# Seven products for the gate and up halves in all four layers, weight sums by adding transfers, result sums in a pre-filled bank

## The chip, the cores and the metric

One Trainium2 chip, and of it one core. The metric is the device time of one execution in microseconds (us). A core has five engines that run beside each other: TensorE (PE) multiplies matrices, VectorE (DVE) and ScalarE (ACT) work element by element, GpSimd (POOL) does small vector work and can issue transfers, SyncE (SP) issues the transfers from main memory. PSUM is the accumulator that TensorE writes: eight banks of 128 x 512 floats. SBUF is the on-chip store that all engines read.

## What is computed

A stack of four layers over 512 tokens of 1024 channels, in float32. Each layer has a mixer (attention and the like), a norm, and a feed-forward part. Only the feed-forward part matters here. Layers 0 and 1 use the first form, layers 2 and 3 the second:

```
def _swiglu(x, w_gate, w_up, w_down):                 # layers 0, 1
    g = jnp.einsum('bsd,df->bsf', x, w_gate)          # 1024 -> 2816
    u = jnp.einsum('bsd,df->bsf', x, w_up)
    return jnp.einsum('bsf,fd->bsd', jax.nn.silu(g) * u, w_down)

def conv_ffn(h, w_up, cw, cb, w_down):                # layers 2, 3
    gu = causal_dwconv(h @ w_up, cw, cb)              # 3 taps along the tokens, per channel
    g, u = jnp.split(gu, 2, axis=-1)
    return (jax.nn.gelu(g, approximate=True) * u) @ w_down
```

## The kernel before

**Arithmetic.** Every product is made of three passes on TensorE: an operand is split into a high half (rounded to the matmul's type) and a low half (the rest), and high x high, high x low and low x high are summed. A block of weights of 128 x 1024 (512 KB) is loaded by SP into a `wraw` buffer (six of them); ScalarE casts it to `whi` (L245), VectorE subtracts to get `wlo` (L246), both with four buffers. `fm` makes one output tile of 128 channels by some tokens from such a block: 8 steps of 128 rows, three passes each, 24 matmuls.

**Layers 2 and 3** use `ffn` (L1308 on): 22 tiles f of 128 hidden channels, each a gate and an up product over 512 tokens, so 44 products of 24 matmuls of 512 columns. For each of the two, ScalarE scales and adds the bias (L1332, Identity), VectorE adds the two shifted taps (L1334, twice); then ScalarE applies Gelu (L1337) and VectorE multiplies (L1338). The first two tiles go through `early`, in halves of 256 tokens, so that they can start before the last tokens are normed.

**Layers 0 and 1** use `quartered`: two neighbouring tiles and both halves of the tokens form a 2 x 2 block problem, in which blocks b11, b12, b21, b22 of the weights meet a11, a12, a21, a22 of the activations, and seven products take the place of eight. There are 11 such units in a layer. One product is 24 matmuls of 256 columns (two groups of 12). Products 1, 2 and 3 use the blocks b11, b21 and b22 as loaded; 4 to 7 use sums of blocks, made by four VectorE additions of 128 x 1024 in each unit (L524). Results gather in three banks, and VectorE forms their differences (L590 to L608) before `finish` applies Silu and the product (L550).

**The seven activation operands** of such a layer are made by `crossed`, one token tile t of 128 at a time: TensorE transposes the normed tile, VectorE and ScalarE split it. For t = 2 and 3, which are the second half of the tokens, the sums of both halves are made and split too (L478 to L487): nine VectorE steps of 128 x 512 for each. This runs at the end of the mixer's last product, beside the norm, and reaches into the first products of the feed-forward part: the work of the last tokens is put off (`later`) and issued behind the third product.

**What sets the order.** There is no planner: each engine executes what is written for it, in program order, and waits on semaphores for what it needs. SP's loads are issued in program order as `wraw` buffers come free. In a unit of layers 0 and 1 the products come as 1, 5, then 3 and 4 of the unit before, 7, 2, 6. No transfer is issued by POOL; POOL computes the power -1/2 of the norms (L410, L1362, on 128 x 1 elements).

Of the kernel before, what the change touches and what calls it, by code (L numbers as in the profile page):

```python
# [30 lines left out]
PAD = 56  # L31
LAG = 1
# [14 lines left out]
BANKS = {"mm": 2, "o": 1, "sc": 3, "tp": 2}  # L47
TOKEN_BANKS = (("mm", "mm"), ("o", "tp"), ("tp", "sc"), ("sc", "sc"))
# [61 lines left out]
def layouts(a):  # L110
# [35 lines left out]
    for l in range(2):  # L146
# [34 lines left out]
        w = a["ffn_up_2"][l].reshape(KD, P, 2, KF, P).transpose(3, 2, 1, 0, 4)  # L181
        o["up" + q] = w
# [7 lines left out]
class Kernel:  # L190
# [60 lines left out]
    def raw(self):  # L251
        return self.tl("wraw", [P, 1024], F32, 6)

    def weights(self, src, shape, piece=False, steps=1):
# [45 lines left out]
    def early(self, srcs, x):  # L300
# [3 lines left out]
        for n, src in enumerate(srcs):  # L304
            ws.append(self.weights(src, [P, KD, P]))
# [141 lines left out]
    def crossed(self, x, t, ops):  # L447

        nc = self.nc
        self.room_for(t, ops)
        tok = slice(P * (t % 2), P * (t % 2) + P)
        ps = []
        for b in range(2):
            ps.append(self.bank(TOKEN_BANKS[t][b]))
            for j in range(4):
                k = 4 * b + j
                nc.tensor.transpose(ps[b][:, P * j:P * j + P], x[:, P * k:P * k + P], self.ident)  # L460
        v = [p.rearrange("p (a b) -> p a b", a=4) for p in ps]

        def parts(n, src):
            hi, lo = ops[n]
            self.split(hi[:, :, tok], lo[:, :, tok], src)

        if t < 2:
            for b in range(2):
                parts(b, v[b])
                nc.scalar.copy(ops["sum"][b][:, :, tok], v[b])  # L470
            return
        sub = nc.vector.tensor_sub
        a11, a12 = (s[:, :, tok] for s in ops["sum"])
        new = lambda: self.tl("kf", [P, 4, P], F32, 3)
        c21 = new()
        nc.scalar.copy(c21, v[0])
        y = self.tl("rt", [P, 4, P], F32, 2)
        sub(y, c21, v[1])  # L478
        parts(3, y)
        d = new()  # L480
        sub(d, a11, c21)
        parts(4, d)
        b = new()
# [29 lines left out]
    def quartered(self, l, ops):  # L513
# [38 lines left out]
        def unit(u):  # L552
# [15 lines left out]
            def q5(again=False):  # L568
                if again:
                    s["b11"] = load(u, 1, 1)  # L570
# [923 lines left out]
```

## Time and profile before

| | |
|---|---|
| time, median of 3 runs | 2358.83 us (2358.7 to 2359.26) |
| profiled execution, its own time | 2359.08 us |
| its span in the profile | 2357.4 us |
| TensorE busy | 2319.1 us, 98% of the span |
| VectorE busy | 1484.8 us, 63% |
| ScalarE busy | 1030.4 us, 44% |
| GpSimd busy | 65.9 us, 3% |

The profile is one execution. "L246" is line 246 of the kernel before. A row of a timeline gives the start, the time and the instruction; neighbouring instructions of an engine overlap a little in these rows, so what one costs in a chain is the distance from its start to the next one's. "PEclk" is the clock that TensorE was granted, 1.00 being 2.4 GHz. A row "wraw<-in_up SPq ... 512.0 KB, 3.4" tells that transfers of 512 KB took 3.4 us from issue to landing, in the median.

### The profile page before, as it was taken

How to read it: one execution, taken by the hardware profiler on the slowest of the kernel's cores; microseconds unless marked ns; L12 is line 12 of the kernel's file. 1: busy time of each engine (PE TensorE's matmuls, PEld its weight loads, DVE VectorE, ACT ScalarE, POOL GpSimd, SP SyncE). 2: the span in 40 equal slices, each digit the busy share in tenths (PEclk: the TensorE clock that was granted, in tenths of full speed). 3: DMA queues.
4: the chain of work that ended last, by engine and by line, in shares of the span. 5: the costliest groups of instructions: out<-in, count | busy, mean ns of one | idle time of the engine just before them, and what ended most of it. 6: DMA issues, size and time to landing. Idle time of an engine off the chain costs nothing.

```text
span 2357.4 us, 33155 instructions
## 1 busy us (share of the span) xinstructions
PE 2319.1 (98%) x13098; PEld 1943.6 (82%) x13098; DVE 1484.8 (63%) x2638; ACT 1030.4 (44%) x1821; POOL 65.9 (3%) x86
## 2 busy tenths in 40 slices
PE   9999899999999989999999999999999999999998
PEld 8668899988977789998888578888888848888887
DVE  5675988735355589885368666556346866655533
ACT  4574544433354554443343554334333364433432
POOL 1001000000000010000010000000000000000000
PEclk9999999999999999999999999999999999999999
DMA  6121333431333113333323213322332322332230
GB/s 204 45 93 65 109 107 101 143 116 46 108 108 99 58 63 117 108 114 128 117 71 112 84 59 117 99 98 94 96 107 73 117 65 80 108 98 95 93 107 36
DMA packets 73979, 227.37 MB, mean 96 GB/s; under 512 B 10712, under 2 KB 13656, under 8 KB 73824
## 3 DMA queue, kind: packets, MB, share of 16 engines
q1 hardware_dynamic: 73824, 225.25, 29.5%
q8 instruction: 103, 1.69, 0.3%
q14 instruction: 52, 0.43, 0.1%
HBM read 218.81 MB, written 2.11 MB: 94 GB/s over the span
## 4 chain that ended last, share of the span: by engine, by line
PE 90%; DVE 6%; ACT 1%; issue 1%; DMA 1%; POOL 1%; SPq 0%; DVEq 0%; POOLq 0%; ACTq 0%
PE sc L281 29%; PE mm L281 28%; PE tp L281 19%; PE o L281 11%; PE tp L709 2%; DVE xl L246 1%; DVE wlo L246 1%; DVE pr L678 0%; ACT rt L400 0%; DVE x L1364 0%; POOL lst L1362 0%; DVE pr L1387 0%; DMA rope<-cum_rows 0%; POOL pst L410 0%; DVE pr L699 0%
## 5 line engine op out<-in xcount | busy, mean ns | idle before, releaser
L246 DVE TENSOR_TENSOR wlo<-wraw,whi 128x1024 fp32r<-128x1024 f32 (+5 forms) x391 | 457.5, 1173 | 611.9 <-ACT whi L245 606.4
L245 ACT CAST whi<-wraw 128x1024 fp32r<-128x1024 f32 (+4 forms) x389 | 394.0, 1015 | 784.1 <-PE sc L281 413.5
L281 PE MATMUL mm<-xh,whi 128*128 128x256 f32 (+2 forms) x912 | 305.2, 335 | 3.9 <-ACT q L561 3.7
L281 PE MATMUL mm<-xh,wlo 128*128 128x256 f32 (+2 forms) x912 | 304.7, 334 | 0.0
L281 PE MATMUL mm<-xl,whi 128*128 128x256 f32 (+2 forms) x912 | 302.9, 332 | 1.1 <-DVE xl L246 1.1
L281 PEld LDWEIGHTS mm<-xh,whi 128*128 128x128 f32 (+1 forms) x912 | 173.5, 190 | 25.2 <-issue 4.8
L281 PEld LDWEIGHTS mm<-xh,wlo 128*128 128x128 f32 (+1 forms) x912 | 173.4, 190 | 18.8 <-issue 2.6
L281 PEld LDWEIGHTS mm<-xl,whi 128*128 128x128 f32 (+1 forms) x912 | 173.6, 190 | 17.9 <-DVE xl L246 1.5
L281 PE MATMUL sc<-xh,wlo 128*128 128x512 f32 (+1 forms) x416 | 145.3, 349 | 8.2 <-DVE wlo L246 8.2
L281 PE MATMUL sc<-xl,whi 128*128 128x512 f32 (+1 forms) x416 | 145.0, 348 | 1.4 <-DVE xl L246 1.4
L281 PE MATMUL sc<-xh,whi 128*128 128x512 f32 (+1 forms) x416 | 144.8, 348 | 0.0
L281 PE MATMUL tp<-xh,whi 128*128 128x256 f32 (+1 forms) x416 | 135.0, 325 | 0.0
L281 PE MATMUL tp<-xl,whi 128*128 128x256 f32 (+1 forms) x416 | 134.7, 324 | 0.0
L281 PE MATMUL tp<-xh,wlo 128*128 128x256 f32 (+1 forms) x416 | 134.7, 324 | 0.0
L694 ACT ACTIVATE pr<-pr,mx 128x512 f32<-128x512 f32 (+3 forms) x160 | 88.3, 555 | 68.2 <-DVE mx L692 68.2
L281 PE MATMUL sc<-pr,whi 128*128 128x256 f32 x352 | 99.8, 284 | 0.0
L281 PE MATMUL sc<-pr,wlo 128*128 128x256 f32 x352 | 99.6, 283 | 0.0
L281 PEld LDWEIGHTS sc<-xh,wlo 128*128 128x128 f32 x416 | 80.7, 194 | 17.8 <-DVE wlo L246 8.6
L281 PE MATMUL sc<-whi,pr 128*128 128x512 f32 x288 | 92.7, 389 | 0.0
L281 PEld LDWEIGHTS sc<-xl,whi 128*128 128x128 f32 x416 | 80.6, 194 | 11.2 <-DVE xl L246 1.8
L281 PEld LDWEIGHTS sc<-xh,whi 128*128 128x128 f32 x416 | 80.7, 194 | 9.3
L281 PE MATMUL sc<-whi,pt 128*128 128x512 f32 x264 | 85.2, 389 | 0.0
(467 smaller groups left out, 5290.0 us busy)
## 6 DMA issues: line engine op xcount, KB each, us to landing
wraw<-in_up SPq DMA_DIRECT2D x180, 512.0 KB, 3.4
wraw<-in_down SPq DMA_DIRECT2D x88, 512.0 KB, 3.4
wraw<-in_i_fm SPq DMA_DIRECT2D x20, 512.0 KB, 3.4
wraw<-in_c_fm SPq DMA_DIRECT2D x16, 512.0 KB, 3.5
wraw<-in_out SPq DMA_DIRECT2D x16, 512.0 KB, 3.5
wraw<-in_i_tok SPq DMA_DIRECT2D x16, 326.0 KB, 2.8
wraw<-in_a_out SPq DMA_DIRECT2D x8, 512.0 KB, 3.3
wraw<-in_c_out SPq DMA_DIRECT2D x8, 512.0 KB, 3.4
```

Source lines behind the costliest of these rows:

```text
L245: nc.scalar.copy(hi, src)
L246: nc.vector.tensor_sub(lo, src, hi.bitcast(F32))
L281: self.last_mm = self.nc.tensor.matmul(out, a, b, start=start, stop=stop, **k)
L694: nc.scalar.activation(prt[t], prt[t], AF.Exp, bias=mx[:, 1, t:t + 1], scale=scale, accum_out=mx[:, 2, t:t + 1])
L709: nc.tensor.transpose(ps[:, at:at + P], prt[t][:, P * kt:P * kt + P], self.ident)
```

## The change

- `ffn` is gone; layers 2 and 3 call `quartered` too, and their norm now makes the seven operands (`crossed`) instead of one.
- Of the sums of weights one is left to VectorE: t1 = b11 + b12, in `sums` (L616). The other three are made in place in a `wsum` buffer (three of them, 128 x 1024), into which b12 is loaded by SP: GpSimd issues a transfer that adds block 22 to it for product 7, one that adds 11 for product 6, and one that adds 21 for product 4 (`added`, L620). Each waits until the product before it has split the sum (ScalarE's cast and VectorE's subtract, now L248 and L249), and the next split waits until it has landed.
- Blocks 11, 21 and 22 are thus read twice from memory in each unit (seven transfers of 512 KB instead of four), and `wraw` has three buffers instead of six.
- Product 1 goes to a bank "mm"; ScalarE writes minus that into a bank "sc" (L603), and products 6, 5 and 3 are added on top of it; ScalarE copies the bank after 6 and after 5. For the first three units of a layer one more matmul of 512 columns is made in that bank ahead of ScalarE's write. VectorE is left with two subtractions of bank results in each unit instead of four.
- `convolved` (L566 to L586) is the ending for layers 2 and 3: the halves are kept in SBUF (by ScalarE's copies or VectorE's subtractions of 128 x 256, L572), and when both are there, the taps (L582), Gelu and the product (L586) follow as before.
- The products of a unit come in the order 7, 4 of the unit before, 6, 3 of the unit before, 5, 2, 1 of the unit after, followed by the t1 of the unit after.
- In `crossed` the operands of t = 2, 3 are made in another order, with the results of the transposes read from the bank: 4, 5, 3, 2, 6.
- `whi` and `wlo` get 1056 columns, and the products of 256 columns use columns 16 to 1039 of them (`SHORT`): their data begin 64 bytes further on.

```diff
+SHORT = 16
+CROSS_BANKS = (("mm", "mm"), ("o", "tp"), ("tp", "o"), ("tp", "o"))
     def raw(self):
-        return self.tl("wraw", [P, 1024], F32, 6)
+        return self.tl("wraw", [P, 1024], F32, 3)
+    def halves(self, place):
+        return [self.tl(n, [P, 1056], F32R, 4)[:, place:place + 1024] for n in ("whi", "wlo")]
...
         def product(ps, src, n, first):
-            hi = self.tl("whi", [P, 1024], F32R, 4)
-            lo = self.tl("wlo", [P, 1024], F32R, 4)
+            hi, lo = self.halves(SHORT)
...
+        def q1(u):
+            s = st[u]
+            s["b11"] = load(u, 1, 1)
+            s["a"] = self.bank("mm")
+            product(s["a"], s["b11"], 0, True)
+            s["b"] = self.bank("sc")
+            if u < BANKS["sc"]:
+                x = ops["parts"][0]
+                self.mm(s["b"], x[:, 0, 0:P], x[:, 0])
+            nc.scalar.activation(s["b"], s["a"], AF.Copy, scale=-1.0)
+        def q2(u):
+            s = st[u]
+            product(s["a"], load(u, 2, 1), 1, False)
+            finish(2 * u, 0, s["a"])
+        def sums(u):
+            s = st[u]
+            s["x"] = load(u, 1, 2, self.tl("wsum", [P, 1024], F32, 3))
+            s["t1"] = self.tl("rope" if u % 2 else "m", [P, D])
+            b11 = load(u, 1, 1) if u < 2 else s["b11"]
+            nc.vector.tensor_tensor(s["t1"], b11, s["x"], op=ALU.add)
+        def added(u, i, j):
+            x = st[u]["x"]
+            nc.gpsimd.dma_start(x, block(u, i, j), accum_op=ALU.add)
+            return x
+        def q7(u):
+            s = st[u]
+            x = added(u, 2, 2)
+            s["c"] = self.bank("tp")
+            product(s["c"], x, 4, True)
+        def q6(u):
+            s = st[u]
+            product(s["b"], added(u, 1, 1), 5, False)
+            s["m"] = self.tl("kf", [P, S], F32, 3)
+            nc.scalar.copy(s["m"], s["b"])
+        def q5(u):
+            s = st[u]
+            product(s["b"], s["t1"], 3, False)
+            n = self.tl("q", [P, S], F32, 4)
+            nc.scalar.copy(n, s["b"])
+            finish(2 * u + 1, 1, None, (n, s["c"]))
+        def q3(u):
+            s = st[u]
+            product(s["b"], load(u, 2, 2), 6, False)
+            finish(2 * u + 1, 0, s["b"])
+        def q4(u):
+            s = st[u]
+            product(s["c"], added(u, 2, 1), 2, False)
+            finish(2 * u, 1, None, (s["c"], s["m"]))
...
         for l in (2, 3):
-            xt = self.parts()
-            use = self.post(xs, f"post{l}", self.pre(f"fpre{l}", xt))
+            ops = self.operands()
+            use = self.post(xs, f"post{l}", self.pre(f"fpre{l}", lambda v, i: self.crossed(v, i, ops)))
...
-            at = self.ffn(xt, l)
+            at = self.quartered(l, ops)
```

On VectorE, in the middle of layer 2, two tiles before stood as follows (L1334 the taps, L1338 the gate product, L246 the low half of a block):

```order
L246 TENSOR_TENSOR wlo_13739<-wraw_13737,whi_13738 128x1024
L1334 SCALAR_TENSOR_TENSOR q_13653<-tp_13591,s_fc_2048_13335,q_13653 128x511
L1334 SCALAR_TENSOR_TENSOR q_13653<-tp_13591,s_fc_2048_13335,q_13653 128x510
L246 TENSOR_TENSOR wlo_13769<-wraw_13767,whi_13768 128x1024
L1334 SCALAR_TENSOR_TENSOR q_13657<-sc_13592,s_fc_2048_13335,q_13657 128x511
L1334 SCALAR_TENSOR_TENSOR q_13657<-sc_13592,s_fc_2048_13335,q_13657 128x510
L1338 TENSOR_TENSOR room_a_13330<-q_13653,q_13657 128x512
L246 TENSOR_TENSOR wlo_13811<-wraw_13809,whi_13810 128x1024
```

Now VectorE has this there, from the split for product 1 of the next unit (first row) over those for product 7 (third row) and product 4 to that for product 6 of the unit (last row); `wsum` is the block that the transfers add to, L582 the taps, L586 the gate product, L572 the subtractions of 256 columns:

```order
L249 TENSOR_TENSOR wlo_14709<-wraw_14705,whi_14708 128x1024
L586 TENSOR_TENSOR room_a_13100<-q_14556,q_14560 128x512
L249 TENSOR_TENSOR wlo_14745<-wsum_14738,whi_14744 128x1024
L582 SCALAR_TENSOR_TENSOR q_14629<-pct_14422,s_fc_2010_13269,q_14629 128x511
L582 SCALAR_TENSOR_TENSOR q_14633<-room_a_13100,s_fc_2010_13269,q_14633 128x511
L582 SCALAR_TENSOR_TENSOR q_14629<-pct_14422,s_fc_2010_13269,q_14629 128x510
L582 SCALAR_TENSOR_TENSOR q_14633<-room_a_13100,s_fc_2010_13269,q_14633 128x510
L572 TENSOR_TENSOR pct_14669<-q_14667,tp_14496 128x256
L586 TENSOR_TENSOR room_a_13100<-q_14629,q_14633 128x512
L572 TENSOR_TENSOR room_a_13100<-q_14667,tp_14496 128x256
L249 TENSOR_TENSOR wlo_14774<-wsum_14491,whi_14773 128x1024
L249 TENSOR_TENSOR wlo_14815<-wsum_14738,whi_14814 128x1024
```

What moved: the low halves stood one for each product of 512 columns, each from a plain load; three of seven now come from `wsum`, and product 6's comes from the buffer that product 7's came from, eight small steps and one split earlier.

On VectorE, at the start of layer 2's feed-forward part, the steps before the first full-width block were few (xl: low half of transposed tokens; L1388: the norm's scaling):

```order
L246 TENSOR_TENSOR xl_12914<-tp_13316,xh_12913 128x4x128
L1403 SCALAR_TENSOR_TENSOR x_1647<-kf_13291,pst_13293,x_1647 128x512
L1403 SCALAR_TENSOR_TENSOR x_1647<-kf_13292,pst_13293,x_1647 128x512
L1387 TENSOR_TENSOR pr_13311<-x_1647,m_12915 128x512 x2
L409 TENSOR_SCALAR pst_13304<-pst_13304 128x1
L246 TENSOR_TENSOR xl_12914<-sc_13323,xh_12913 128x4x128
L1388 TENSOR_SCALAR pr_13311<-pr_13311,pst_13304 128x512 x2
```

Now the operands of the token tiles t = 2 and 3 stand there. These are those of t = 3, with the split for product 7 of unit 0 (`wlo_13442`) and, as the last row, that for product 6 of unit 0:

```order
L249 TENSOR_TENSOR piece_13236<-rt_13261,pr_13235 128x4x128
L504 TENSOR_TENSOR rt_13382<-room_a_13100,tp_13372 128x512
L249 TENSOR_TENSOR wlo_13442<-wsum_13400,whi_13441 128x1024
L249 TENSOR_TENSOR pt_13232<-rt_13382,pr_13231 128x4x128
L508 TENSOR_TENSOR kf_13386<-rt_13382,o_13377 128x512
L504 TENSOR_TENSOR rt_13390<-room_a_13100,kf_13386 128x512
L504 TENSOR_TENSOR rt_13396<-room_a_13100,kf_13386 128x512
L249 TENSOR_TENSOR pt_13234<-kf_13386,pr_13233 128x4x128
L249 TENSOR_TENSOR xl_12824<-rt_13390,xh_12823 128x4x128
L249 TENSOR_TENSOR xl_12824<-o_13377,xh_12823 128x4x128
L249 TENSOR_TENSOR piece_13236<-rt_13396,pr_13235 128x4x128
L249 TENSOR_TENSOR wlo_13477<-wsum_13400,whi_13476 128x1024
```

What moved: twenty steps of VectorE, t1 of units 0 and 1 (L616) among them, stand between the norm's last scaling and the split for product 6, and the splits for products 7 and 6 each wait for an adding transfer.

POOL had no transfer before; now its queue has, behind the norm's last power in layer 2, the adding transfers in this order (three for each `wsum` buffer: blocks 22, 11 and 21):

```order
L416 TENSOR_TENSOR pst_13219<-pst_13219,mhalf 128x1
L620 DMA wsum_13400<-in_up 128x1024
L620 DMA wsum_13469<-in_up 128x1024
L620 DMA wsum_13400<-in_up 128x1024 x2
L620 DMA wsum_13469<-in_up 128x1024
L620 DMA wsum_13750<-in_up 128x1024
L620 DMA wsum_13469<-in_up 128x1024
```

What moved: the queue was empty from there to the end of the feed-forward part, and each of these waits for a split on ScalarE and VectorE.

## Rows read from the trace of the kernel before

**Rows 1.** The profile's first page: busy time of each engine; chain that ended last.

```profile
PE 2319.1 (98%) x13098; PEld 1943.6 (82%) x13098; DVE 1484.8 (63%) x2638; ACT 1030.4 (44%) x1821; POOL 65.9 (3%) x86
...
PE 90%; DVE 6%; ACT 1%; issue 1%; DMA 1%; POOL 1%; SPq 0%; DVEq 0%; POOLq 0%; ACTq 0%
```

**Rows 2.** Windows, gate and up part of layers 0, 1, 2, 3 (columns: first row).

```profile
core 0: us, PE busy (x) PEld busy (x) DVE busy (x) ACT busy (x) POOL busy (x), PEclk, DMA share, GB/s
224.07:458.94 234.87, 227.91 (x1870) 226.44 (x1869) 208.13 (x250) 119.60 (x166) 2.49 (x2) 0.99 0.35 113
845.70:1077.43 231.73, 224.79 (x1846) 223.32 (x1846) 205.40 (x245) 117.22 (x163) 2.31 (x2) 0.99 0.35 114
1415.08:1656.72 241.64, 241.64 (x1163) 204.19 (x1162) 140.14 (x170) 96.91 (x124) 1.09 (x2) 1.00 0.31 103
1989.10:2230.80 241.70, 241.70 (x1163) 204.31 (x1162) 140.16 (x170) 96.97 (x124) 1.09 (x2) 1.00 0.31 101
```

**Rows 3.** Windows: a unit of layer 0; four tiles of layer 2; layer 0's start; 0 to 50.

```profile
294.16:314.32 20.16, 20.16 (x170) 20.16 (x169) 17.36 (x21) 9.85 (x14) 0.00 (x0) 1.00 0.33 106
1444.56:1488.08 43.52, 43.52 (x193) 36.04 (x193) 23.84 (x28) 16.36 (x21) 0.00 (x0) 1.00 0.31 99
224.07:250.39 26.32, 19.36 (x138) 18.27 (x136) 25.44 (x38) 15.59 (x26) 2.49 (x2) 0.87 0.21 63
...
0.00:50.00 50.00, 47.08 (x241) 42.02 (x242) 26.26 (x51) 22.10 (x44) 5.44 (x12) 1.00 0.67 224
```

**Rows 4.** Pieces of the chain, layer 1: start, us, what; 24 matmuls of 256 columns.

```profile
1053.34 2.88 PE mm L281 x24
```

**Rows 5.** The same view, layer 2: 24 matmuls of 512 columns.

```profile
1645.84 5.44 PE o L281 x24
```

**Rows 6.** The same view, start of layer 2's feed-forward part (L440: transposes).

```profile
1413.56 0.50 DVE pr L1388
...
1415.19 5.75 PE mm L281 x48
1420.95 2.88 PE o L281 x24
1423.83 0.87 PE sc L440 x8
1424.70 2.87 PE tp L281 x24
```

**Rows 7.** TensorE's timeline, start of layer 0: matmuls after idle time (last bracket).

```profile
237.32 0.39 PE L281 MATMUL mm<-xh,whi 128*128 128x256 f32 x1 [1.84 <-ACT q L561]
...
241.25 0.38 PE L281 MATMUL sc<-xl,whi 128*128 128x256 f32 x1 [0.69 <-DVE xl L246]
...
245.73 0.58 PE L281 MATMUL sc<-xh,wlo 128*128 128x256 f32 x1 [4.09 <-DVE wlo L246]
```

**Rows 8.** VectorE's timeline, layer 0: neighbouring starts give the cost of each form.

```profile
233.04 1.28 DVE L1364 SCALAR_TENSOR_TENSOR x<-x,lst,m 128x1024 f32<-128x1024 f32 x1 [0.44 <-POOL lst L1362]
234.24 0.68 DVE L484 TENSOR_TENSOR kf<-room_a,rt 128x512 f32<-128x512 f32 x1
...
239.31 0.68 DVE L481 TENSOR_TENSOR kf<-room_a,kf 128x512 f32<-128x512 f32 x1
239.92 0.68 DVE L484 TENSOR_TENSOR kf<-room_a,rt 128x512 f32<-128x512 f32 x1
...
249.07 1.22 DVE L524 TENSOR_TENSOR m<-wraw,wraw 128x1024 f32<-128x1024 f32 x1
250.21 1.22 DVE L246 TENSOR_TENSOR wlo<-rope,whi 128x1024 fp32r<-128x1024 f32 x1
```

**Rows 9.** VectorE's timeline elsewhere: 256 columns; the two taps; the norm's scaling.

```profile
302.30 0.42 DVE L550 TENSOR_TENSOR room_a<-rt 128x256 f32<-128x256 f32 x1
302.63 0.68 DVE L608 TENSOR_TENSOR rt<-tp,kf 128x512 f32<-128x512 f32 x1
...
1452.04 1.53 DVE L1334 SCALAR_TENSOR_TENSOR q<-sc,s_fc,q 128x511 f32<-128x511 f32 x2
...
1421.11 0.88 DVE L1388 TENSOR_SCALAR pr<-pr,pst 128x512 f32<-128x512 f32 x2
```

**Rows 10.** Transfers: tile and source, queue, count, KB, median us from issue to landing.

```profile
wraw<-in_up SPq DMA_DIRECT2D x180, 512.0 KB, 3.4
...
wraw<-in_c_vc SPq DMA_DIRECT2D x8, 256.0 KB, 2.6
...
wraw<-in_a_uv SPq DMA_DIRECT2D x1, 512.0 KB, 8.2
```

**Rows 11.** Groups of POOL's instructions by line: busy us, mean ns, idle before.

```profile
L1362 POOL TENSOR_TENSOR lst<-lst,mhalf 128x1 f32<-128x1 f32 x16 | 24.7, 1542 | 1030.7 <-DVE lst L1361 1030.7
L410 POOL TENSOR_TENSOR pst<-pst,mhalf 128x1 f32<-128x1 f32 x32 | 17.5, 548 | 822.0 <-DVE pst L409 799.5 <-ACT whi L245 10.6 <-ACT xh L245 8.4
```

**Rows 12.** Chain pieces around 617: products of 260 columns, 24 between first and last.

```profile
616.96 0.72 PE mm L281 x6
...
619.84 0.72 PE mm L281 x6
```

**Rows 13.** ScalarE's timeline, layer 2: the cast of a block, then the next instruction.

```profile
1444.37 1.05 ACT L245 CAST whi<-wraw 128x1024 fp32r<-128x1024 f32 x1 [3.11 <-PE tp L281]
```

More of the change, by code (lines that the diff above doesn't have):

```diff
@@ L444, in transposed @@
             self.split(hi, lo, v)
[L447 to L483, printed above, removed]
-        sub(b, a11, y)
-        parts(5, b)
-        e = self.tl("rt", [P, 4, P], F32, 2)
-        sub(e, a12, b)
-        parts(6, e)
-        parts(2, v[1])
     def operands(self):
@@ L511, in room_for, with crossed, parts, summed @@
             ops[n] = [f()[:, 0:1024].bitcast(F32R).rearrange("p (a b) -> p a b", a=4) for f in (pr, low)]
+    def crossed(self, x, t, ops):
+        nc = self.nc
+        self.room_for(t, ops)
+        tok = slice(P * (t % 2), P * (t % 2) + P)
+        ps = []
+        for b in range(2):
+            ps.append(self.bank(CROSS_BANKS[t][b]))
+            for j in range(4):
+                k = 4 * b + j
+                nc.tensor.transpose(ps[b][:, P * j:P * j + P], x[:, P * k:P * k + P], self.ident)
+        v = [p.rearrange("p (a b) -> p a b", a=4) for p in ps]
+        def parts(n, src):
+            hi, lo = ops[n]
+            self.split(hi[:, :, tok], lo[:, :, tok], src)
+        if t < 2:
+            for b in range(2):
+                parts(b, v[b])
+                nc.scalar.copy(ops["sum"][b][:, :, tok], v[b])
+            return
+        a11, a12 = (s[:, :, tok] for s in ops["sum"])
+        def summed(n, tag, bufs, f, *of):
+            s = self.tl(tag, [P, 4, P], F32, bufs)
+            f(s, *of)
+            parts(n, s)
+            return s
+        sub, add = nc.vector.tensor_sub, lambda o, a, b: nc.vector.tensor_tensor(o, a, b, op=ALU.add)
+        d = summed(4, "rt", 2, sub, a11, v[0])
+        b = summed(5, "kf", 3, add, d, v[1])
+        summed(3, "rt", 2, sub, a11, b)
+        parts(2, v[1])
+        summed(6, "rt", 2, sub, a12, b)
     def quartered(self, l, ops):
@@ L613, in quartered, with gated @@
-        units = [unit(u) for u in range(KF // 2)]
-        q = lambda u, n, *k: units[u][n - 1](*k)
-        q(0, 1)
-        q(0, 2)
-        q(1, 1)
+        def gated(f, half, c, minus=None):
+            s = self.tl("pct", [P, S]) if minus is None else self.tl("rt", [P, S], F32, 2)
+            if minus is not None:
+                sub(s, *minus)
+                c = s
+            nc.scalar.activation(s[:, 0:256], c[:, 0:256], AF.Silu)
+            nc.vector.tensor_tensor(at(f)[:, 256 * half:256 * half + 256], c[:, 256:512], s[:, 0:256], op=ALU.mult)
@@ new lines, in quartered @@
+        finish = gated if l < 2 else convolved
+        st = [{} for _ in range(last + 1)]
+        def q1(u):
[12 more added lines that the diff above has]
+            finish(2 * u, 0, s["a"])
@@ L637, in quartered @@
-        q(KF // 2 - 1, 3)
-        q(KF // 2 - 1, 4)
+        sums(0)
+        q2(1)
+        q7(0)
+        sums(1)
+        q6(0)
+        q5(0)
+        for u in range(1, last + 1):
+            q7(u)
+            q4(u - 1)
+            q6(u)
+            q3(u - 1)
+            q5(u)
+            if u > 1:
+                q2(u)
+            if u < last:
+                q1(u + 1)
+                sums(u + 1)
+        q4(last)
+        q3(last)
         return at
```

165 lines of the change are left out of this document (46 added, 119 removed).

## The prediction

> **What bounds the kernel now.** I read the page first: TensorE is busy 98% of the span and holds 90% of the chain that ended last; VectorE is at 63% and ScalarE at 44% [rows 1]. So a change gains only by shortening TensorE's own work or its idle gaps, and loses by making it wait. The windows over the four gate and up parts come next: 234.87 and 231.73 us in layers 0 and 1, 241.64 and 241.70 in layers 2 and 3 [rows 2]. In layers 2 and 3 TensorE is never idle; in 0 and 1 it is idle about 7 us. Inside, a unit of layer 0 takes 20.16 us with TensorE full and VectorE at 17.36; four tiles of layer 2 take 43.52, so two tiles (a unit's worth) take 21.76 [rows 3]. The pieces of the chain show why: 24 matmuls of 256 columns take 2.88 us (120.0 ns each), 24 of 512 take 5.44 [rows 4, 5]. Seven times 2.88 is 20.16, four times 5.44 is 21.76. The idle time of layer 0 stands at its start, in three gaps of 1.84, 0.69 and 4.09 us, where TensorE waits for VectorE [rows 7]; the mean granted clock there is 0.87 [rows 3], a stretch of about 7 us on the lower level (1.2 GHz) after these gaps.
>
> The sum is made against the profiled execution, 2359.08 us (span 2357.4, so 1.7 lie outside it); the median of the runs is 2358.83, 0.25 below. 0.2% of this, 4.7 us, is about what a measurement here can tell from no change.
>
> **Step 1: fewer products in layers 2 and 3.** 21.76 - 20.16 = 1.60 us for each unit, on the path, 11 units, two layers: 35.2 us. With 77 products of 2.88 a layer would take 221.8, plus some 1.1 for the transposes between them (0.87 for eight [rows 6]): 222.9 instead of 241.7, if TensorE never waited. That is 18.8 for each layer and more than 17.6, since `early` had cost four products of 512 columns some extra.
>
> **Step 2: the start of these layers.** Here the gain meets a chain that was not there. Before, TensorE went through the start of layer 2 with no gap: 48, 24, 24 matmuls and eight transposes from 1415.19 on [rows 6], because VectorE had only low halves to make. Now VectorE makes the operands of t = 2 and 3, t1 of unit 0 stands among them, and product 7 needs a transfer that GpSimd can issue only after that t1. Let L be the time from issue to landing of an adding transfer. The norm's last scaling ends at 1421.99 [rows 9]; then two steps of 512 columns (0.60 each from start to start) and t1 (1.14) [rows 8]: 1424.3. Block 22 lands at 1424.3 + L, ScalarE casts it in 1.05 [rows 13], VectorE makes the low half in 1.14. GpSimd then adds block 11 to the same buffer for product 6: L, 1.05 and 1.14 again. So product 6 of unit 0 can start at about 1424.3 + 2L + 4.4, less 0.3 since its first two matmuls need only the high half.
>
> **What L is.** No adding transfer is in the trace. The nearest row is the plain load of 512 KB, 3.4 us; 256 KB take 2.6 [rows 10], so a pass of 512 KB costs 2 x 0.8 = 1.6 and the rest, 1.8, is fixed. An addition has to fetch the block and the destination, which I count as a second pass: 3.4 + 1.6 = 5.0. Four plain loads in a unit keep the transfer engines busy a third of the time (DMA share 0.33 [rows 3]), so a third of 1.6 us of waiting: L = 5.5, an estimate. The ends are 3.4 (no dearer than a plain load) and 8.2 (the slowest 512 KB load of the trace [rows 10], in the crowded first 50 us, where the share is 0.67 at 224 GB/s [rows 3]). Below 3.4 nothing points, as the bytes are the same.
>
> With 5.5, product 6 starts at 1439.4. Products 1, 2, 1, 2 and the transposes from 1415.1 and product 7 right after them would let it start at 1430.5. So 8.9 us are lost; two more for the lower clock after two gaps of 3 us or more (about 4.4 of layer 0's 7 us fall behind its last gap, at half speed [rows 3, 7]). Layers 2 and 3 end up at 222.9 + 10.9 = 233.8, close to what layers 0 and 1 take now, 7.9 less than before: **-15.8** for both. Each us of L costs 2 us in each layer, from L = 4.2 on; below, VectorE's own steps decide the first wait.
>
> **Step 3: the start of layers 0 and 1.** The same chain takes the place of a shorter one. Before, product 5 of unit 0 waited for VectorE until 245.73 [rows 7] and the rest ran without a gap. Now: the norm's last step ends at 234.24 [rows 8]; then seven steps of 512 columns, one of 256 (0.33 [rows 9]) and t1: 234.24 + 4.2 + 0.33 + 1.14 = 239.9. Block 22 lands at 245.4, product 7 starts at 246.5, block 11 is issued at 247.6, lands at 253.1, and product 6 starts at about 255. Before, the second product after the gap began near 250. So **+5** for each layer, **+10**; 2 us for each us of L. Steps 2 and 3 together: -5.8, say **-5**, as the fresh loads of three blocks stand close together there.
>
> **Step 4: the steady loop.** The engines that feed TensorE have room. VectorE, by unit of layers 2 and 3: eight steps of 1024 columns (1.14), eight taps (0.72), four of 256 (0.33), two of 512 (0.60): 17.4 of 20.16. In layers 0 and 1 it loses three additions and two subtractions. The loop that can bind is block 11: after product 7's split GpSimd adds, ScalarE casts, VectorE splits, then does t1, four more splits, the taps and product 7's split of the next unit. Those are 1.05 + 1.14 + 6 x 1.14 + 2.9 (taps) + 0.67 + 0.60 = 13.2 of work, so a unit takes at least 13.2 + L; this hides under 20.16 up to L = 7.0. Cost 0 at 5.5; uncovered it is 1 us per unit and us of L. GpSimd's queue holds these transfers in order; behind a waiting one stand only the next ones, until the norm, whose powers come when all have gone. Three `wraw` buffers give 3 x 2.88 = 8.6 us to a load that lands in 3.4: 0. The banks filled by ScalarE cost a copy of 0.6 us in its idle half: 0. The twelve further matmuls of 512 columns (0.23 each) fall into the gaps: 0, at most +3. Three loads of `wsum` blocks that fall in the first 50 us would take 7 us at 224 GB/s: 0 where TensorE is 94% busy, at most +7.
>
> **Step 5: the shifted columns.** 4 x 77 x 24 = 7392 matmuls of 256 columns read weights 64 bytes further on. In before all of them are on round addresses and take 120.0 ns. The nearest row with other steps is the product of 260 columns: 24 matmuls from 616.96 to 619.84, again 120.0 [rows 12], so four more columns cost nothing. Scaled to 256 columns that is 118.2 ns: -1.8 ns x 7392 = **-13**. The ends: no effect, 0; transposes of 128 columns come every 109 ns (0.87 for eight [rows 6]), and if the gap between matmuls shrank to that, -11 ns, -81 us. A loss isn't excluded: the 260-column rows have single spacings up to 125 ns, which over all would be +37; their mean of 120.0 makes this unlikely.
>
> **Sum:** 2359.1 - 5 - 13 = **2341**.
>
> **A rule against the change.** L1362 on POOL takes 1542 ns, L410, with the same shape, 548 [rows 11]; the former runs beside VectorE's long steps with two SBUF inputs. If issuing a transfer were held up likewise, L would be 6.5 and the time 2341 + 8 = 2349. The Trainium skill, SBUF — State Buffer, section "Who interferes with whom", says that a GpSimd instruction that reads SBUF is blocked beside such a VectorE step, which agrees with these two rows, but that one that only writes is not, and that descriptors (written by GpSimd) starve only beside VectorE's two-port modes; by it L stays 5.5 in the loop and the time 2341. No row here shows which.
>
> **The rivals.** *Quicker matmuls* (0.17): the shift removes a third to all of the 11 ns; between 2280 and 2330, say 2300 for 5 to 6 ns. For it: a matmul of 256 columns takes 6.7 ns more than half of one of 512 (5.44 / 24 = 0.2267 us [rows 5]), so each has some time that isn't its columns. Against it: the 260-column rows. *Quick additions* (0.12): L = 3.4, transitions 15 us shorter, 2326. *No difference* (0.13): the shift does nothing; at L = 5.5 to 6 the starts eat the gain: 2354 to 2358. *Late additions* (0.22, the slower side): the loop of step 4. With seven transfers for four the engines' share rises from 0.33 to 0.58, to 0.83 if an addition counts twice, near the level at which the slowest load took 8.2. At L = 8: starts +20, and 13.2 + 8 - 19.9 = 1.3 us in each of some nine units of two layers, +24: 2385. It turns slower from L = 7.0 on; with matmuls of 120 ns, from 6.1.
>
> **How the numbers follow.** The forecast case has 0.36 and 2330 to 2352; the chances: faster 0.36 + 0.17 + 0.12 less a little for its upper edge = 0.64; same 0.14; slower 0.22. The range has to take in most of the quick and the late cases: 2290 to 2386.
>
> **What the profile of the changed kernel would show.** Steps 2 and 3: TensorE idle at product 7 and at product 6 of unit 0, each released by the cast or split of a block from `wsum`, some 9 us in all in layers 2 and 3; those two parts at about 234, layers 0 and 1 at about 240 and 237, each less 3 for step 5. Step 4: units of 19.9 to 20.2 us with TensorE full, in all four layers. Step 5: 24 matmuls in 2.84. The row for `wsum<-in_up` gives L: 5.5. I am wrong if that row says 7 or more, if units of layers 2 and 3 take over 20.2, or if 24 matmuls take 2.7 or less.

## The result and the profile after

The changed kernel takes 2379.6 us (median of four runs, 2373.93 to 2383.45) against 2358.91 before: 1.0086 times as long, 95% interval 1.0065 to 1.0106. It is slower by 21 us, where 18 us less were forecast; the time lies inside the range and on the wrong side. The profiled execution has a span of 2377.9 us, 20.5 more than before.

First the page of the changed kernel (the lines that answer to [rows 1] and [rows 10]; in the transfer rows: tile and source, queue, count, KB, median us from issue to landing):

```profile
PE 2282.9 (96%) x14502; PEld 1959.8 (82%) x14502; DVE 1505.1 (63%) x2710; ACT 1159.5 (49%) x2079; POOL 183.4 (8%) x218
...
PE 70%; DMA 13%; DVE 8%; issue 5%; ACT 3%; POOL 1%; SPq 0%; POOLq 0%; DVEq 0%; ACTq 0%
...
wraw<-in_up SPq DMA_DIRECT2D x140, 512.0 KB, 4.7
wsum<-in_up POOLq DMA_DIRECT2D x132, 512.0 KB, 5.7
```

TensorE has 36 us less to do, and the chain that ended last holds 70% of it instead of 90%; 13% of the chain are now transfers into `wsum`. Their median landing, 5.7 us, is what the prediction had put (5.5). So the estimate was right for most transfers; the median hides those that took 8 us and more, which are shown below. The windows tell in which layer (changed kernel, gate and up parts of layers 0 to 3, from the first to the last product of 256 columns, to compare with [rows 2]):

```profile
core 0: us, PE busy (x) PEld busy (x) DVE busy (x) ACT busy (x) POOL busy (x), PEclk, DMA share, GB/s
...
224.51:460.93 236.42, 220.47 (x1868) 217.64 (x1866) 152.45 (x184) 118.89 (x173) 30.88 (x35) 0.96 0.76 181
849.61:1084.12 234.51, 220.94 (x1867) 218.20 (x1866) 152.27 (x184) 118.78 (x173) 30.51 (x35) 0.96 0.77 184
1422.27:1667.66 245.39, 225.84 (x1861) 220.34 (x1859) 201.60 (x266) 156.58 (x236) 31.00 (x35) 0.97 0.71 172
2000.80:2249.05 248.25, 227.62 (x1862) 221.83 (x1860) 201.75 (x266) 156.78 (x236) 30.58 (x35) 0.97 0.68 162
```

Layers 0 and 1 take 236.4 and 234.5 us, where they took 234.9 and 234.5 before (layer 1's window in [rows 2] ends one product early). Layers 2 and 3 take 245.4 and 248.3 instead of 241.6 and 241.7, where 231 had been forecast. With layer 0's 1.6 that is 11.9 us; the other 8.6 of the 20.5 lie outside the gate and up parts, where the prediction had put nothing.

The chain in layer 0's steady part (changed kernel; start, us, what) answers to [rows 4]:

```profile
311.23 8.16 PE sc L287 x72
319.39 5.44 PE mm L287 x48
324.83 5.44 PE tp L287 x48
```

A product of 24 matmuls takes 2.72 us here, 113.3 ns for each, and a unit 168 x 113.3 = 19.04 us, with TensorE full. The shifted columns thus bring 6.7 ns, not 1.8. In layer 2 the same view shows no TensorE at all (changed kernel, one unit):

```profile
1499.78 0.84 POOL wsum L620
1500.62 0.13 issue
1500.75 8.97 DMA wsum<-in_up
...
1509.80 1.06 ACT whi L248
...
1510.89 1.24 DVE wlo L249
1512.12 0.35 issue
1512.47 5.22 DMA wsum<-in_up
...
1520.47 0.85 POOL wsum L620
1521.31 0.26 issue
1521.57 8.71 DMA wsum<-in_up
```

The transfer at 1500.75 adds block 22 for the next product 7: 8.97 us. Cast and low half follow, then the transfer of block 11 at 1512.47 (5.22), its cast and split, the next t1, and the next block 22 at 1521.57. A unit is 1521.57 - 1500.75 = 20.82 us, and two adding transfers, one behind the other, are 14 of it. GpSimd's timeline (changed kernel, layer 2; start, us, instruction, idle before it and what ended that) shows why block 22 takes 8.97:

```profile
1562.16 0.88 POOL L620 DMA_DIRECT2D wsum<-in_up  x1 [7.32 <-DVE wlo L249]
1563.30 0.88 POOL L620 DMA_DIRECT2D wsum<-in_up  x1 [0.26 <-issue]
1576.18 0.88 POOL L620 DMA_DIRECT2D wsum<-in_up  x1 [12.00 <-DVE wlo L249]
```

At 1562.16 it issues block 21 of the unit, which nobody needs soon, and 1.1 us behind it block 22 of the next, which product 7 waits for. The one issued first lands after 5.2 to 6 us, the one behind it after 8.4 to 10.1 (the units from 1490 to 1650). In layers 0 and 1 the built program has another order (changed kernel, layer 0: block 11, block 22 of the next unit, block 21):

```profile
300.22 0.88 POOL L620 DMA_DIRECT2D wsum<-in_up  x1 [10.55 <-DVE room_a L559]
303.23 0.88 POOL L620 DMA_DIRECT2D wsum<-in_up  x1 [2.13 <-DVE m L616]
308.62 0.88 POOL L620 DMA_DIRECT2D wsum<-in_up  x1 [4.51 <-DVE room_a L559]
```

There t1 (`m`, 301.64 to 302.87) stands on VectorE ahead of product 6's split (307.03), not behind it as in layer 2. So block 22 goes 3 us behind block 11 and ahead of block 21. It lands after 6.1 us (6.1 to 7.7 in the units from 300 to 440), and ScalarE casts it only at 316.60: some 7 us are to spare.

So one sentence ahead of the prediction was wrong. "There is no planner" doesn't hold: what builds the program reorders the instructions, as the same code stands in different order in layers 0 and 2. In the code block 22 of a unit (`q7`) stands ahead of block 21 of the unit before (`q4`). Layers 0 and 1 and the first units of layers 2 and 3 have it so; from block 21 of unit 3 on, layers 2 and 3 have it the other way round.

### The profile page after: what moved, and what is told of

Read it like the earlier page. It is cut to its first block, busy times and chain, and to the rows that moved or that the text cites. A ratio compares the mean times of both kernels' runs of the same rounds, so it can differ in the third digit from the quotient of the medians.

```text
span 2377.9 us, 36882 instructions
## 1 busy us (share of the span) xinstructions
PE 2282.9 (96%) x14502; PEld 1959.8 (82%) x14502; DVE 1505.1 (63%) x2710; ACT 1159.5 (49%) x2079; POOL 183.4 (8%) x218
## 4 chain that ended last, share of the span: by engine, by line
PE 70%; DMA 13%; DVE 8%; issue 5%; ACT 3%; POOL 1%; SPq 0%; POOLq 0%; DVEq 0%; ACTq 0%
PE mm L287 23%; PE sc L287 22%; PE tp L287 14%; DMA wsum<-in_up 13%; PE o L287 8%; PE tp L746 2%; DVE wlo L249 2%; ACT whi L248 1%; DVE xl L249 1%; POOL wsum L620 1%; DVE x L1367 0%; DVE pr L715 0%; DVE pr L1390 0%; POOL pst L416 0%; ACT rt L1362 0%
## 5 line engine op out<-in xcount | busy, mean ns | idle before, releaser
L249 DVE TENSOR_TENSOR wlo<-wraw,whi 128x1024 fp32r<-128x1024 f32 (+5 forms) x325 | 376.8, 1162 | 418.9 <-ACT whi L248 409.4
L248 ACT CAST whi<-wraw 128x1024 fp32r<-128x1024 f32 (+4 forms) x323 | 323.7, 1004 | 543.7 <-PE sc L287 338.1
L287 PE MATMUL mm<-xh,whi 128*128 128x256 f32 (+1 forms) x1040 | 320.4, 308 | 4.3 <-ACT sc L603 4.1
L287 PE MATMUL mm<-xh,wlo 128*128 128x256 f32 (+1 forms) x1040 | 319.7, 307 | 0.0
L287 PE MATMUL mm<-xl,whi 128*128 128x256 f32 (+1 forms) x1040 | 317.9, 306 | 1.1 <-DVE xl L249 1.1
L249 DVE TENSOR_TENSOR wlo<-wsum,whi 128x1024 fp32r<-128x1024 f32 x132 | 161.5, 1223 | 190.7 <-ACT whi L248 190.7
L248 ACT CAST whi<-wsum 128x1024 fp32r<-128x1024 f32 x132 | 138.4, 1048 | 271.2 <-DMA wsum<-in_up 198.9
L287 PEld LDWEIGHTS mm<-xh,whi 128*128 128x128 f32 x1040 | 195.7, 188 | 20.9 <-ACT sc L603 6.0
L287 PEld LDWEIGHTS mm<-xh,wlo 128*128 128x128 f32 x1040 | 195.8, 188 | 12.6 <-issue 2.6
L287 PEld LDWEIGHTS mm<-xl,whi 128*128 128x128 f32 x1040 | 195.7, 188 | 11.9 <-DVE xl L249 1.5
L620 POOL DMA_DIRECT2D wsum<-in_up x132 | 115.5, 875 | 741.8 <-DVE wlo L249 414.4
L287 PEld LDWEIGHTS sc<-pr,whi 128*128 128x128 f32 x704 | 135.0, 192 | 24.6 <-ACT sc L603 14.0
L287 PEld LDWEIGHTS sc<-pr,wlo 128*128 128x128 f32 x704 | 135.2, 192 | 7.3 <-DVE wlo L249 7.3
```

Of the source, the lines that this page charges most:

```text
L248: nc.scalar.copy(hi, src)
L249: nc.vector.tensor_sub(lo, src, hi.bitcast(F32))
L287: self.last_mm = self.nc.tensor.matmul(out, a, b, start=start, stop=stop, **k)
L620: nc.gpsimd.dma_start(x, block(u, i, j), accum_op=ALU.add)
```

## The experiments

Two questions stand: what the shifted columns are worth by themselves, and what makes layers 2 and 3 late. The theory on the second is the loop above, closed by block 22's place in GpSimd's queue; its rivals are VectorE's remaining work, and the starts of the parts. Each expectation names its theories by letters of its own.

**The shift alone.** The kernel before, with `whi` and `wlo` of 1088 columns of which `early` and the gate and up products leave the first 16 free; at its core:

```diff
-            hi = self.tl("whi", [P, 1024], F32R, 4)
-            lo = self.tl("wlo", [P, 1024], F32R, 4)
+            hi, lo = self.halves(SHORT)
```

> The kernel before, with one thing of the change: the weights of its products of 256 columns begin 64 bytes further on (whi and wlo of 1088 columns, so that every buffer begins on a multiple of 256 bytes). Theory A (the address alone makes a matmul of 256 columns take 113.4 ns instead of 120.0): its 3696 matmuls in layers 0 and 1 and 960 in `early` save 6.6 ns each, 30.7 us, so 2328 us, units of layers 0 and 1 at 19.04. Theory B (the quicker matmuls of the changed kernel come from its order of products or its banks): 2359 us, units at 20.16.

2340.4 us, 0.9916 times the time before (0.9897 to 0.9934). The address alone does it: layer 1 takes 222.7 us instead of 234.5. It is 12 us short of theory A, and the chain shows where (run before_shift, layer 1 and layer 0):

```profile
995.79 2.72 PE mm L285 x24
998.51 2.72 PE sc L285 x24
1001.23 2.72 PE mm L285 x24
```

```profile
345.16 2.83 PE mm L285 x24
347.99 2.83 PE sc L285 x24
350.81 2.83 PE mm L285 x24
```

The same code on the same addresses runs at 113.3 ns in layer 1 and at 117.8 in layer 0. It stays with one of the two for many products. In the trace of the changed kernel each change to the slower pace stands next to a pause of TensorE or to matmuls of another form; most changes back stand next to neither. A layer of 1848 matmuls at the slower pace is 8 us longer. The two paces may also be why the runs of this kernel scatter by 11 us (2332.97 to 2343.69), where those of the kernel before beside them lie within 3.5; that isn't shown, since run after_even, below, scatters by 7.5 us without shifted columns.

**The padding alone.** The kernel before with `whi` and `wlo` of 1056 columns and nothing shifted.

> The kernel before with whi and wlo of 1056 columns and nothing shifted, so that the four buffers begin at 0, 128, 256 and 384 bytes within 512. Theory A (products of 512 columns are slower, 232 ns instead of 227, when their weights begin at 128 or 384): half of some 5300 matmuls of 512 columns lose 5 ns, 13 us: 2372 us. Theory B (the 232 ns of the changed kernel come from its busier transfers): 2359 us.

2371.8 us, 1.0051 times the time before (1.0036 to 1.0066), as theory A had it. 1056 columns are 4224 bytes, so of the four buffers two begin at 128 and 384 bytes within 512. In the products of 512 columns (run before_pad, chain; seven matmuls each) both prices stand, 1.63 / 7 = 233 ns and 1.59 / 7 = 227, as the buffers take turns:

```profile
2275.40 1.63 PE sc L285 x7
...
2286.34 1.59 PE sc L285 x7
```

The matmuls of 256 columns, which this run doesn't shift, now have two prices too, 120.0 ns and 2.85 / 24 = 118.8 (run before_pad, chain, layer 0):

```profile
305.59 2.88 PE mm L285 x24
308.47 2.85 PE sc L285 x24
```

So 64 bytes is not the only distance that leaves 120.0 ns, though nothing without the shift comes near 113.3 for a whole product.

**The changed kernel without this loss.** `[P, 1056]` becomes `[P, 1088]`.

> The changed kernel with whi and wlo of 1088 columns instead of 1056, so that each buffer begins on a multiple of 256 bytes. Theory A (the address): some 1500 matmuls of 512 columns outside the gate and up parts go back from 232 to 227 ns, 7 us: 2372 us. Theory B (busier transfers): 2380.

2370.8 us, 1.0045 (1.0031 to 1.006): 9 us less, and a median of 227 ns again for the matmuls of 512 columns. The 8.6 us outside the gate and up parts are explained: the padding of the weights' buffers slows the other products. Without it these parts take 1404.0 us, as before (1404.7; 1413.3 in the changed kernel). The next kernels start from this one.

**The changed kernel without the shift.**

> The changed kernel with nothing shifted (SHORT 0, whi and wlo of 1024 columns). Theory A (in layers 2 and 3 a unit waits for two adding transfers in a row and is not bound by TensorE; in layers 0 and 1 it is bound by TensorE): units of layers 0 and 1 go from 19.04 to 20.16, +25; units of layers 2 and 3 stay at about 21; matmuls of 512 columns gain 7: 2397 us. Theory B (TensorE bounds all four): +49 - 7, 2421 us.

2390.3 us, 1.0134 (1.0119 to 1.0149). Without the shift layers 0 and 1 take 247.4 and 246.1 us (after_wide: 240.2 and 235.7), but layers 2 and 3 take 243.0 and 243.4, hardly another time than with it (242.5 and 246.6). What TensorE gains for each matmul is not seen there: theory A. This run gives one more number. At equal spacing layers 0 and 1 are 12.8 and 11.6 us longer than before, where the prediction had put 5 for the start.

**Block 21's transfer left out in layers 2 and 3.**

```diff
-            product(s["c"], added(u, 2, 1), 2, False)
+            product(s["c"], added(u, 2, 1) if l < 2 else s["x"], 2, False)
```

> The kernel of run after_wide without the adding transfers of block 21 in layers 2 and 3 (product 4 there takes the sum without block 21, so its result is left incomplete). Theory A (block 22 of the next unit lands late, after 8.5 to 9 us, because it is issued 1.1 us behind block 21's adding transfer): its landing falls to 5.5 to 6.5, units of layers 2 and 3 go from about 20.9 to 19.1, -34 us: 2337 us. Theory B (it lands late because of the three plain loads that SP issues at the same moment): landing stays over 8, units at 20.8: 2370 us.

2354.9 us, 0.9987 (0.9977 to 0.9997). From unit 4 on block 22 now lands after 6.0 to 7.5 us, and TensorE is full in layer 2 (run no_21, chain):

```profile
1561.68 8.16 PE sc L287 x72
1569.84 5.44 PE mm L287 x48
1575.28 5.44 PE tp L287 x48
```

The two layers become 10.3 and 10.4 us shorter, less than the 17 expected; in units 0 to 3 block 22 still lands after 7.6 to 10.2 us. The wait goes as theory A says; but the run also takes away a seventh of the bytes, so it doesn't tell order from amount. Run queue, below, does.

**t1 and block 22 ahead of product 6**, by the order of the code.

```diff
             q4(u - 1)
+            if u < last:
+                sums(u + 1)
+                x7(u + 1)
             q6(u)
```

> The kernel of run after_wide with t1 and block 22's adding transfer of the next unit written ahead of product 6, so that they leave the loop from product 6's split over t1 and block 22 to product 7's split. All transfers stay. Theory A (that loop, with two adding transfers in a row, sets the 20.9 us of a unit in layers 2 and 3): units at 19.04 to 19.2, 2337 us. Theory B (the transfer engines have too much to do with seven transfers for four): units stay over 20.5 wherever the transfers stand, 2370 us.

2488.7 us, 1.055 (1.0533 to 1.0568), which neither theory had. The waits of VectorE (run ahead, layer 0, 300 to 420: engine, what waited for what, us in total, times, longest; L620 is t1 in this kernel) point to a flaw of the experiment:

```profile
DVE wlo L249 <- ACT whi L248: 30.1, 16, 4.8
DVE rope L620 <- DMA wraw<-in_up: 12.9, 3, 4.4
DVE m L620 <- DMA wraw<-in_up: 8.1, 2, 4.6
```

t1 needs block 11, which is then held for product 1, so one of three `wraw` buffers is kept for most of a unit, the next block 11 can only be loaded late, and VectorE stands 21 us behind the t1 that waits for it. That this is what costs the time is argued and not shown: the wait for ScalarE's casts is longer, and these wait 21.2 us for adding transfers themselves. The run says nothing on the loop; it suggests that three `wraw` buffers are no cost only in the order they were chosen for.

**Unit 0's sums for products 7 and 6 on VectorE**, in all layers.

```diff
-            x = added(u, 2, 2)
+            x = on_vector(u, 2, 2) if u < 1 else added(u, 2, 2)
```

(and the same for block 11).

> The kernel of run after_wide with the sums for products 7 and 6 of unit 0 made by VectorE from plain loads, in all four layers; the later units as they were. Theory A (the start of each layer waits for two adding transfers in a row, 7.7 and 5.3 us with a cast behind each): the gaps ahead of products 7 and 6 shrink by 8 to 10 us in each layer: 2371 - 36 = 2335 us. Theory B (VectorE is late there anyway, and unit 1's transfers come next): under 3 us in each, 2360 us or more.

2360.5 us, 1.0014 (0.9998 to 1.003): 10 us for four layers, theory B. TensorE's waits at the start of layer 1 (run start_on_vector, timeline; the bracket is the idle time before and its releaser):

```profile
863.11 0.39 PE L287 MATMUL mm<-xh,whi 128*128 128x256 f32 x1 [1.45 <-ACT sc L603]
...
873.39 0.58 PE L287 MATMUL tp<-pr,whi 128*128 128x256 f32 x1 [6.74 <-ACT whi L248]
...
875.19 0.58 PE L287 MATMUL tp<-pr,wlo 128*128 128x256 f32 x1 [1.00 <-DVE wlo L249]
...
883.38 0.38 PE L287 MATMUL tp<-pr,whi 128*128 128x256 f32 x1 [0.31 <-ACT whi L248]
...
891.66 0.39 PE L287 MATMUL sc<-pr,whi 128*128 128x256 f32 x1 [1.52 <-ACT whi L248]
```

Product 7 still waits 6.7 us, for VectorE's chain over the operands of both token tiles and two sums; product 6 doesn't wait any more, and unit 1 waits for its own transfers.

**Both, and product 6's sum always on VectorE.**

> Both: t1 and block 22 of the next unit ahead as in run ahead, unit 0 on VectorE as in run start_on_vector, and the sum for product 6 made by VectorE in all units (adding transfers are left for block 22 and block 21). Theory A: the two gains add up, 2371 - 34 - 36 = 2301 us, units of all layers at 19.04. Theory B (VectorE, with 18.5 us of work for a unit in layers 2 and 3, becomes the bound): units of 19.5 to 20, 2310 to 2325 us.

2360.7 us, 1.0003 (0.9994 to 1.0012), which neither theory had. Layers 0 and 1 take 244.0 and 246.1 us; there VectorE still waits 21 us for the block 11 that t1 needs (300 to 440). But layers 2 and 3 take 232.5 and 231.1 us, less than in any other run that leaves no transfer out. TensorE is full there, with VectorE at 92% (run ahead_both, layer 2, columns as in [rows 2]):

```profile
1520.00:1600.00 80.00, 80.00 (x682) 80.00 (x681) 73.92 (x93) 55.91 (x83) 7.03 (x8) 1.00 0.72 186
```

A unit takes 19.79 us, 168 matmuls at the slower pace of 117.8 ns. So in these layers the loop can also be opened by moving t1 and block 22 ahead of product 6, with product 6's sum on VectorE; run ahead alone, with that sum left to a transfer, took 275 us for each of them. Which of its two further edits made the difference is not told apart.

**Only the order in GpSimd's queue.** After_wide with one edge more (an order between two instructions that the builder has to keep):

```diff
+                with self.tc.issue_after(st[u + 1][2, 2].ins):
+                    x = added(u, 2, 1)
```

> The kernel of run after_wide with one edge more: block 21's adding transfer is issued behind the next unit's block 22 in GpSimd's queue (in layers 2 and 3 it stood ahead of it). Every transfer and every step of the other engines stays, in the same order. Theory A (block 22 lands late for standing 1.1 us behind block 21, and product 7 waits for it): block 22 lands after 5.5 to 6, block 21 after 8 to 9, units of layers 2 and 3 at 19.1 to 19.6, -14 us for each of the two layers: 2343 us. Theory B (it lands late for the amount of transfers in flight): units stay near 20.8, 2370 us.

2361.2 us, 1.0005 (0.9995 to 1.0015). All transfers are there. GpSimd's timeline (run queue, layer 2), to set beside the one above:

```profile
1566.52 1.78 POOL L620 DMA_DIRECT2D wsum<-in_up  x2 [9.05 <-DVE rope L616]
1576.11 0.88 POOL L620 DMA_DIRECT2D wsum<-in_up  x1 [7.81 <-DVE wlo L249]
1586.13 1.80 POOL L620 DMA_DIRECT2D wsum<-in_up  x2 [9.14 <-DVE m L616]
```

Block 22 now goes at 1566.52, as soon as t1 is made, with block 21 in its shadow. It lands after 6.4 us (up to 8.6 in the units before), block 21 after 9.6 to 11.4. A unit takes 1586.13 - 1566.52 = 19.61 us instead of 20.8 and more, layers 2 and 3 take 237.0 and 234.1 (242.5 and 246.6 in after_wide). So it is the order: theory A. The whole time fell by 10 us and not by the 28 expected: the two layers gave 18, and layer 0 ran at the slower of the two paces in this execution (243.8 against 240.2).

**The two old layers old, the two new ones mended.** Layers 0 and 1 as in before_shift, layers 2 and 3 as in queue with unit 0 on VectorE.

> Layers 0 and 1 as in run before_shift (four sums on VectorE, the old order of products and operands, blocks 21 and 22 in the wsum buffers), layers 2 and 3 as in run queue with unit 0's sums for products 7 and 6 on VectorE; buffers of 1088 columns. Theory A (in layers 0 and 1 the old form starts 10 to 12 us earlier, in layers 2 and 3 the new one gains once its loop is broken): layers 0 and 1 at 231 and 223, layers 2 and 3 at 225 to 230 against 241.7: 2340 - 28 = 2312 us. Theory B (three wraw buffers are too few for the old form, or layers 2 and 3 stay at 240): 2335 to 2345 us.

2336.5 us, 0.9911 (0.9894 to 0.9927). It beats both kernels, and before_shift by 4 us, less than the scatter of either. The time lies in theory B's range, but layers 2 and 3 lie between the two theories: 235.9 and 233.3 us against 241.7 before. So the seven products are worth some 14 us there, shift included, not 35. In this trace nearly all of layer 3 ran at the slower pace, which is some 7 us of it.

**Product 6's sum on VectorE too**, in layers 2 and 3; and besides it block 22 of unit 1.

> The kernel of run mixed with the sum for product 6 made by VectorE in all units of layers 2 and 3 (adding transfers are left for blocks 22 and 21, 21 behind the next 22). Theory A (the loop over blocks 22 and 11, 6.4 and 6 us, still sets 19.5 us of a unit there; without block 11 it is about 18): units of layers 2 and 3 bound by TensorE at 19.04 to 19.8, starts 3 to 5 us shorter: 2336 - 14 = 2322 us. Theory B (VectorE, 18.5 us of work for a unit and waits of its own, takes over as the bound): units over 19.8, 2336 us or more.

> The kernel of run mixed_six with block 22 of unit 1 added by VectorE too, so that no product before the fourth of unit 1 waits for a transfer. Theory A (the wait for unit 1's block 22 is still on the path at the start of layers 2 and 3): 2 to 4 us less in each of the two, 2316 us. Theory B (VectorE's own steps are last there): within 2 us of run mixed_six.

2343.5 us, 0.9933 (0.9918 to 0.9948), and 2348.7, 0.9947 (0.9932 to 0.9962): theory B for the first; the second is 5 us longer still, which neither of its theories had. The same 80 us of layer 2 in run mixed and run mixed_six (columns as in [rows 2]):

```profile
1520.00:1600.00 80.00, 80.00 (x683) 79.93 (x682) 69.21 (x89) 55.81 (x83) 10.65 (x12) 1.00 0.77 188
```

```profile
1520.00:1600.00 80.00, 77.65 (x670) 76.61 (x669) 73.78 (x93) 55.11 (x81) 7.12 (x8) 1.00 0.71 187
```

With VectorE at 92% TensorE waits again (7.8 us from 1480 to 1640: 4.1 for ScalarE's copy of a bank, 3.7 for VectorE); with the transfers it was full. But VectorE's share alone doesn't decide that: in run ahead_both it is 92% too, product 6's sum is on VectorE as well, and TensorE is full. So product 6's adding transfer is worth its trouble in the order of run mixed; where t1 and block 22 go ahead of product 6, layers 2 and 3 did better without it.

## Why the prediction was wrong

**Steps 1 and 5, TensorE's work: the mechanism right, step 5 mis-sized.** Seven products do replace eight. The shift was worth 6.7 ns for each matmul, or 2.2 in stretches at the slower pace, not 1.8: the 260-column rows [rows 12] change the number of columns and leave the weights where they were, so scaling by columns had no ground. Of the two ends that were given, none and 11 ns, the truth lies past the middle. By itself it would be -31 us in the kernel before (6.7 ns for each matmul of the seven products in layers 0 and 1, 6.6 for those of `early`), of which before_shift realized 18.8. This error was to the good side, and it is why layers 0 and 1 came out near the forecast although their starts cost more: two errors that cancel, which is luck.

**Missed: the buffers' padding.** The diff shows 1056 columns, and the prediction spoke only of the 64 bytes inside. The other products' weights lie at the start of the same buffers, and two of four moved to 128 and 384 bytes within 512: +8.6 us outside the part that changed (before_pad, after_wide). A layout change has to be followed to everyone who uses the tile.

**What L is: right for a transfer that has none just ahead of it.** Where no other adding transfer was issued in the 4 us before, the median is 5.5 to 5.7 us in each of the four layers, against 5.5. GpSimd's own step took 0.88 us, in layers 0 and 1 with VectorE 65% busy and in layers 2 and 3 with VectorE 82% busy, and these transfers landed equally. So the rule weighed ahead, that issuing would be held up as L1362 was, is not borne out. The Trainium skill, SBUF — State Buffer, section "Who interferes with whom", expects no hold-up beside steps of VectorE like these; by that rule, the trace agrees, with these numbers.

**Step 4, the steady loop: the step that failed.** It took one L for all transfers, counted block 11's in the loop and let block 22's run beside VectorE's work. Step 2 had said that GpSimd can issue block 22 only behind t1, and step 4 itself has t1 behind product 6's split; the two were not put together. So the loop goes through two transfers and not one. What step 4 left for block 22 beside VectorE is 8.7 us (four splits, the taps and two small steps). That block 21 goes ahead of it could not be read from the rows of GpSimd's queue ahead of the prediction: they end with unit 1's block 21, and up to there block 22 of the next unit goes first. Issued 1.1 us behind block 21, block 22 takes 8.9 and is with its cast later than VectorE: 8.97 + 1.06 + 1.24 (cast and split) + 0.35 + 5.22 (block 11) + 1.06 + 1.24, and t1 and the issue steps make up the 20.8 us. With 5.5 for block 22 the same sum is 17.4 and would have hidden; run queue, with 6.4, is at 19.6, and run no_21 at TensorE's own 19.04. The rival of late additions had lateness right and its place and reason wrong: its loop is block 11's alone, which kept its 5.2 to 5.8, and the share of the transfer engines was no lower in run queue (0.75, 1520 to 1600) than in the changed kernel (0.71). That its 2385 came out near 2379.6 is luck; the padding and the quicker matmuls are not in it.

**Steps 2 and 3, the starts: right in kind, too small.** In layers 0 and 1 they cost 12.8 and 11.6 us at equal spacing (run after_even) where 5 had been put. In layer 0 block 22 was issued at 240.36 (239.9 forecast), landed at 248.1 (245.4), and product 6 began at 257.2 (255). In layer 2, where all is 7.3 us later, it began at 1450, 27.7 us after the part's start (24.3 forecast). The first transfer took 7.7 and 7.8 us, beside the burst of loads there. What was not counted in layer 0 is what comes after: unit 1's blocks queue behind unit 0's, so product 6 of unit 1 waits too. TensorE in the first 52 us of layer 0, after and before (two kernels, windows):

```profile
224.51:276.00 51.49, 35.91 (x246) 33.47 (x245) 33.00 (x44) 21.79 (x33) 8.05 (x9) 0.83 0.56 121
```

```profile
224.07:276.00 51.93, 44.97 (x351) 43.88 (x350) 50.59 (x66) 28.75 (x43) 2.49 (x2) 0.93 0.33 106
```

105 matmuls fewer: its waits grew from 7 to 15.6 us, and the granted clock went down with them, 0.83 against 0.93. It was 0.50, the lower level of 1.2 GHz, from 243.2 to 253.4 and from 256.8 to 263.7, around the waits of 8.5 us for product 7 and 2.6 for product 6; before, only from 243.3 to 250.1, around the wait of 4.1. VectorE, which was nearly full there before, is at 33 of 51 us: the transfers took work off it where it was needed and put their own landing in its place.

**The sum.** Against the forecast 2341 the kernel is 39 us late: some 31 in layers 2 and 3 (245.4 and 248.3 against 231), 8.6 from the padding, and in layers 0 and 1 about nothing, since some 7 us more at the start of each met some 8 us less from the quicker matmuls (113.9 ns on average there, 118.2 forecast). Of the 31, run no_21 took 21 back by mending the loop; what the rest is made of, starts and slower matmuls, is not told apart.

**What stays open.** What decides between 113.3 and 117.8 ns is not settled. Of the addresses that were run only the shifted ones gave 113.3 for a whole product (120.0 in after_even, 120.0 and 118.8 in before_pad), and before_shift shows both paces on equal addresses. Why block 22 takes 8.9 us behind block 21 (the queue's own order, or the sharing of the engines by two transfers and three plain loads) is not told apart. It is nothing of block 21 itself: in run no_21 unit 3's block 22, issued 1.1 us behind a block 11, took 10.2.

## What to carry to other kernels

Work that goes from an engine to a transfer changes from a duration into a latency: draw the loop of who waits for whom over one whole period, with every transfer in it, before asking whether an engine has time left. In a queue that works in order, put the transfer that someone waits for ahead of the one that nobody needs yet, and look at the built order in each place where the same code runs. Where a buffer gets a new size or offset, look at the addresses of all buffers behind it and of all their users.

## What the runs showed of the hardware that was not expected

- A matmul of 256 columns takes 120.0 ns with its weights on multiples of 256 bytes (before, after_even) and 113.3 or 117.8 ns with them 64 bytes further on (before_shift, both in one program); it keeps one of the two paces over many products. With two of four buffers at 128 and 384 bytes within 512 and no shift (before_pad), products take 120.0 or 118.8.
- A matmul of 512 columns takes 227 ns with its weights on multiples of 256 bytes and 232 to 233 ns when they begin at 128 or 384 within 512.
- An adding transfer of 512 KB lands after 5.6 us in the median when no other was issued in the 4 us before it from the same queue, after 6.1 to 7.7 us when issued 3 us behind another (layer 0), after 8.2 to 10.5 when issued 1.1 us behind it (layers 2 and 3), and after 9.6 to 11.4 when issued 0.6 us behind it (run queue).
